# The order of loads, sums and gates in the merged stage of a hybrid attention and convolution layer

## The chip, the cores and the metric

The kernel runs on one core of a Trainium2 chip. The metric is the device time of one execution, in microseconds (us). The engines in the text are TensorE (PE for its products, PEld for its weight loads), VectorE (DVE), ScalarE (ACT), GpSimd (POOL) and SyncE (SP). SP does nothing but start transfers; POOL and ACT start some as well.

## The reference

A block of 256 tokens with 2048 channels goes through one layer: a norm, one wide input projection, two token mixers side by side (attention and a short convolution), two gates, and an output projection with a residual.

```
proj = jnp.einsum('bsd,de->bse', h, w_in)       # q_a, c_kv, k_rope, z_mla, c_in, ..., g_mla, g_conv
attn = attn.reshape(b, s, MLA_WIDTH) * jax.nn.silu(z_mla)
y_mla = jnp.einsum('bse,ed->bsd', attn, w_o_mla)
y_conv = jnp.einsum('bse,ed->bsd', b_gate * conv * jax.nn.silu(z_conv), w_o_conv)
merged = jax.nn.sigmoid(g_mla) * y_mla + jax.nn.sigmoid(g_conv) * y_conv
out = jnp.einsum('bsd,de->bse', merged, w_out)
x = x + _rmsnorm(out, post_norm_g)
```

All data are float32. The change touches what comes after the heads of the attention: the gates g_mla (g_m below) and g_conv (g_c), the products with w_o_mla and w_o_conv, and their merging.

## The kernel before

**Splits.** Every float32 operand is split into a high part, which TensorE takes at its rate for rounded numbers, and a low part, what the rounding left. ACT writes the high part (L252), DVE the low part as a subtraction (L253), and each product is three: high with high, high with low, low with high. On the names: raw is a weight tile as loaded, whi and wlo are its parts (half a tile each, so four instructions per tile), shi and slo are the same for a sum of weight tiles.

**Units.** The merged stage, from about 598 us of the span on, is a list, seq, of units. A unit is a load, a split, products and something that follows them. A plain unit loads one weight tile of 128 x 2048 numbers (1 MiB) by load_raw (L164) and makes 24 products of 128 x 128 by 128 x 512. Each of the four matrices g_m (0), g_c (1), w_o_mla (2) and w_o_conv (3) has four column blocks of four tiles. The tiles are numbered: raw113 to raw116 are g_m's column block 0, raw117 to raw120 g_c's, raw121 to raw136 w_o_mla, then w_o_conv, then the output weights.

**Pairs.** For column blocks 1 to 3 both gates are made together, by paired(c): seven products of half the depth in place of eight, out of sums of weight tiles and of sums of the inputs, called forms. The results stand in three PSUM banks, X, Z and Y, and become four gates: a (g_m, first 128 tokens), b (g_c, first), c (g_c, second) and d (g_m, second). The seven, in order, are Q1 (form 11 into X), V5 (form 5 into Z), V6 (form 6 into X), V7 (form 7), V4 (form 22), V3 (form 3) and Q2 (form 12 into Y). Each has two units of 12 products. The weights of a pair come as tiles b<c>_<matrix>_<tile>. Their sums stand on DVE (L1197): V5 adds b_1_0 and b_1_1 to b_0_0 and b_0_1, V6 adds b_1_2 and b_1_3 to the same, V4 adds b_0_2 and b_0_3. V5 also starts two accumulating transfers on POOL (L1201), which add the tiles 2 and 3 of g_c to b_1_0 and b_1_1 in place; V7 uses these. After V6 ACT copies bank X into sb (L1227); sa, sc and sd are the like for a, c and d.

**Between the pairs** stand plain units of w_o_mla: s1 is Q1, unit 121, V5, unit 122, V6, unit 123, V7, unit 124, V4, 125, 126, V3, 127, Q2, 128. Units 121 to 124 also take in the four blocks of the attention's output. These were written to DRAM and come back transposed as turned90_0 to turned90_3 (L1086); their split is at_both0 to at_both3 on ACT and DVE.

**What sets the order.** seq is walked once. At unit j, loads of up to four units behind it are called, then the splits up to two units behind it, then j's products, then what follows them (copy, sum, sigmoid and the store of a gate, L1026). That only records the work. A scheduler with its own model of times then sets the order in which the instructions stand on each engine; instructions inside tc.keep_in_program_order keep the order of the record. PE's matmuls are all kept. SP's loads of the merged stage are not, so the scheduler may take them in another order than that of seq. Each engine then works through its own list strictly in order. Tiles named raw share three buffers; the tags rt, rb and rc of the pairs' tiles have two each.

**The forms** are made earlier, between the heads of the attention, by make_forms; POOL stores them to DRAM (far_form), and bring_form (L1036) loads them back on SP, in seq, a few units ahead of their use.

Of the kernel before, what the change touches and what calls it, by code (L numbers as in the profile page):

```python
# [82 lines left out]
def tile_layer(ctx: ExitStack, tc: tile.TileContext, xw, w0, xb, x, pos, pvec, post_g, wc, wz, wcv, wkr, wqk, wqr, wv, cwr, wsq, xf, out):  # L83
    nc = tc.nc
# [66 lines left out]
    def load_raw(i):  # L151
# [11 lines left out]
        for a, b, piece in pieces:  # L163
            nc.sync.dma_start(out=t[:, a:b], in_=piece)  # L164
# [664 lines left out]
    def make_forms():  # L829

        kq = KH // 2
        for c in range(2):
# [38 lines left out]
            goes = []  # L871
            for n, src, sign, s in (
                ("11", a11, 1.0, None), ("22", a22, 1.0, None), ("12", a12, 1.0, None), ("5", u, 1.0, (u, a22, a21, ALU.subtract)),
                ("6", w, -1.0, (w, u, a11, ALU.add)), ("7", f7, 1.0, (f7, a11, a21, ALU.subtract)),
                ("3", f3, 1.0, (f3, w, a12, ALU.subtract)),
            ):
# [158 lines left out]
    def bring_form(n):  # L1035
        nc.sync.dma_start(  # L1036
            out=form[n][:, :, :, :].rearrange("p k j c -> p (k j c)").bitcast(F32), in_=far_form[n][:, :]
        )


    seq = []
# [36 lines left out]
    def turned_unit(far, both, first, queue=nc.sync):  # L1078
# [4 lines left out]
        def load():  # L1083
            t = wpool.tile([P, UNIT], F32, name=f"turned{len(seq)}_{first}", tag="raw", bufs=3)
            for i, f in enumerate(far):
                queue.dma_start(out=t[:, i * 1024 : (i + 1) * 1024], in_=f[:, :])  # L1086
            box.append(t)
# [93 lines left out]
    def paired(c):  # L1181
# [133 lines left out]
    s2["Q2"][1][3] = lambda: (gate_last(), branch_last())  # L1315
# [53 lines left out]
    for j in range(len(seq)):  # L1369
        ahead_loads = 0  # L1370
        while nl < len(seq):
            if nl > j and seq[nl][0]:
                pass
# [13 lines left out]
        if j + 3 > len(seq) and done["split"] == u_out[0, 0]:  # L1387
# [3 lines left out]
        if seq[j][2]:  # L1391
            seq[j][2](w)
        if seq[j][3]:
            seq[j][3]()

# [202 lines left out]
```

## Time and profile before

| | us |
|---|---|
| median of 3 runs | 1062.15 |
| lowest and highest | 1062.01 and 1063.28 |
| the profiled execution | 1064.04 |
| its span | 1062.3 |

The span is what the trace covers; 1.7 us of the profiled execution lie outside it. Times in the trace count from the start of the span. "Busy" is the sum of an engine's instructions; a wait row names who waited, for whom, the sum, how often and the longest. PEclk is the clock that TensorE was granted, as a share of the full one.

### The profile page before, as it was taken

What the parts mean: (1) busy time and instruction counts of PE and PEld (TensorE: products, weight loads), DVE (VectorE), ACT (ScalarE), POOL (GpSimd) and SP (SyncE); (2) the same over time, 40 slices, a digit from 0 to 9 for tenths busy, and PEclk for the clock granted to TensorE, in tenths of its full rate; (3) what the DMA queues carried; (4) which work ended last, traced back from release to release, by engine and by line L of the source; (5) the groups of instructions that cost most, each with busy time, mean ns of one, the idle gap of its engine ahead of it and who ended that gap; (6) DMA issues with size and microseconds to landing.
All of it is one profiled execution on the core that took longest, in us unless ns stands there. A gap on an engine that the chain in (4) does not pass through costs nothing.

```text
span 1062.3 us, 12896 instructions
## 1 busy us (share of the span) xinstructions
PE 1020.0 (96%) x4576; PEld 843.5 (79%) x4576; DVE 785.3 (74%) x1074; ACT 580.4 (55%) x811; POOL 200.7 (19%) x366
## 2 busy tenths in 40 slices
PE   9999999999999999999999994799999999998997
PEld 7888888878788788888888873588888778887786
DVE  7588978788677786877767833787988988665662
ACT  7666656546456455564655531565667665433551
POOL 4620322203411223112333201000100102142000
PEclk9999999999999999999999998799999999999999
DMA  9776778759776687756777799578778875687742
GB/s 356 284 240 233 276 230 290 253 192 323 250 273 236 197 292 232 248 200 211 279 248 247 249 403 344 197 285 335 210 247 327 236 286 179 238 309 298 293 179 80
DMA packets 55153, 273.13 MB, mean 257 GB/s; under 512 B 9232, under 2 KB 11920, under 8 KB 30512
## 3 DMA queue, kind: packets, MB, share of 16 engines
q1 hardware_dynamic: 35280, 213.30, 55.3%
q0 software_dynamic: 16784, 50.98, 15.9%
q10 hardware_dynamic: 3024, 8.01, 1.9%
q8 instruction: 36, 0.59, 0.2%
q14 instruction: 29, 0.24, 0.1%
HBM read 239.78 MB, written 28.31 MB: 252 GB/s over the span
## 4 chain that ended last, share of the span: by engine, by line
PE 70%; DMA 15%; DVE 8%; issue 4%; ACT 2%; POOL 1%; DVEq 0%; ACTq 0%; POOLq 0%; SPq 0%
PE cv L88 25%; PE sq L88 15%; PE out L88 6%; DMA raw<-wsq_dram 4%; PE z L88 4%; PE sX L88 4%; DMA form<-far_form 3%; DMA far_form<-form 3%; PE sZ L88 3%; DVE wlo L253 2%; PE qa L88 2%; PE ckv L88 2%; DMA cw<-cwr_dram 2%; PE kn L88 2%; PE qn L88 2%
## 5 line engine op out<-in xcount | busy, mean ns | idle before, releaser
L252 ACT ACTIVATE whi<-raw 128x1024 fp32r<-128x1024 f32 (+1 forms) x318 | 324.3, 1032 | 271.8 <-PE cv L88 97.0
L253 DVE TENSOR_TENSOR wlo<-raw,whi 128x1024 fp32r<-128x1024 f32 (+1 forms) x316 | 371.5, 1191 | 135.3 <-ACT whi L252 129.0
L88 PE MATMUL cv<-whi,x_both 128*128 128x512 f32 x1024 | 320.6, 390 | 2.9 <-DVE vv_lo L253 2.9
L88 PEld LDWEIGHTS cv<-whi,x_both 128*128 128x128 f32 x1024 | 192.7, 188 | 43.4 <-DVE vv_lo L253 3.8
L88 PE MATMUL cv<-wlo,x_both 128*128 128x512 f32 x512 | 200.0, 391 | 0.7 <-DVE wlo L253 0.7
L88 PEld LDWEIGHTS cv<-wlo,x_both 128*128 128x128 f32 x512 | 96.4, 188 | 21.0 <-DVE wlo L253 1.6
L88 PE MATMUL sq<-whi,at_both 128*128 128x512 f32 x256 | 83.3, 398 | 20.4 <-ACT whi L252 20.4
L252 ACT ACTIVATE shi_V<-b 128x1024 fp32r<-128x1024 f32 x60 | 62.6, 1058 | 54.5 <-PE sq L88 33.8
L253 DVE TENSOR_TENSOR slo_V<-b,shi_V 128x1024 fp32r<-128x1024 f32 x60 | 71.8, 1222 | 21.0 <-ACT shi_V L252 20.1
L88 PE MATMUL z<-whi,x_both 128*128 128x512 f32 x256 | 79.9, 389 | 0.0
L88 PE MATMUL sq<-whi,cv_both 128*128 128x512 f32 x256 | 79.9, 389 | 0.0
L88 PEld LDWEIGHTS sq<-whi,at_both 128*128 128x128 f32 x256 | 49.5, 193 | 31.3 <-ACT whi L252 20.8
L338 POOL DMA_DIRECT2D far<-via x64 | 35.4, 559 | 185.6 <-DVE via L330 180.5
L88 PE MATMUL out<-whi,m_both 128*128 128x512 f32 x208 | 66.0, 396 | 1.0 <-ACT whi L252 1.0
L88 PEld LDWEIGHTS sq<-whi,cv_both 128*128 128x128 f32 x256 | 48.1, 188 | 10.0
L88 PEld LDWEIGHTS z<-whi,x_both 128*128 128x128 f32 x256 | 48.1, 188 | 9.9
L88 PE MATMUL sq<-wlo,at_both 128*128 128x512 f32 x128 | 51.2, 400 | 0.5 <-DVE wlo L253 0.5
L88 PE MATMUL sq<-wlo,cv_both 128*128 128x512 f32 x128 | 50.1, 391 | 1.6 <-DVE wlo L253 1.6
L88 PE MATMUL z<-wlo,x_both 128*128 128x512 f32 x128 | 49.8, 389 | 0.0
L88 PEld LDWEIGHTS out<-whi,m_both 128*128 128x128 f32 x208 | 39.8, 191 | 9.7 <-ACT whi L252 1.4
L88 PE MATMUL sX<-shi_V,form 128*128 128x512 f32 x144 | 45.8, 389 | 0.0
L88 PE MATMUL out<-wlo,m_both 128*128 128x512 f32 x104 | 41.3, 397 | 3.9 <-DVE wlo L253 3.9
(281 smaller groups left out, 1578.4 us busy)
## 6 DMA issues: line engine op xcount, KB each, us to landing
raw<-wcv_dram SPq DMA_DIRECT2D x64, 1024.0 KB, 5.9
raw<-wsq_dram SPq DMA_DIRECT2D x56, 1024.0 KB, 6.2
b<-wsq_dram SPq DMA_DIRECT2D x24, 1024.0 KB, 5.4
raw<-wz_dram SPq DMA_DIRECT2D x16, 1024.0 KB, 5.2
raw<-wqk_dram SPq DMA_DIRECT2D x8, 1024.0 KB, 6.5
far_form<-form POOLq DMA_DIRECT2D x14, 512.0 KB, 7.8
form<-far_form SPq DMA_DIRECT2D x7, 1024.0 KB, 18.1
cw<-cwr_dram POOLq DMA_DIRECT2D x24, 256.0 KB, 6.1
```

Of the source, the lines that this page charges most:

```text
L88: return tc.keep_in_program_order(nc.tensor.matmul(*a, **kw))
L252: a = nc.scalar.activation(hi, src, AF.Copy)
L253: b = nc.vector.tensor_tensor(lo, src, hi.bitcast(F32), op=ALU.subtract)
L338: tc.keep_in_program_order(queue.dma_start(out=f[i], in_=m))
```

## The change

It has five parts.

- The loads of the merged stage (weights from g_m's first tile on, forms, pair tiles, and the attention's output) are marked to keep the order of the record on SP.
- In make_forms the sum for the next form is recorded behind the split of the present one.
- New is later(n, fn), which records fn after the products of the n-th unit behind the present one. Sums stay with the unit and the sigmoids that read them on ACT are recorded one unit later. For gate c the sum is recorded one and the sigmoid two units later. The product of the third column block with its gate is recorded two units later.
- The early split of the output weights at the end of the walk may take two tiles, not one.
- Unused lines in the walk go.

```diff
@@ load_raw
-            nc.sync.dma_start(out=t[:, a:b], in_=piece)
+            d = nc.sync.dma_start(out=t[:, a:b], in_=piece)
+            if i >= u_d[0][0][0]:
+                tc.keep_in_program_order(d)
@@ make_forms
-                ("11", a11, 1.0, None), ("22", a22, 1.0, None), ("12", a12, 1.0, None), ("5", u, 1.0, (u, a22, a21, ALU.subtract)),
-                ("6", w, -1.0, (w, u, a11, ALU.add)), ("7", f7, 1.0, (f7, a11, a21, ALU.subtract)),
-                ("3", f3, 1.0, (f3, w, a12, ALU.subtract)),
-            ):
-                if s:
-                    tt(*s)
+                ("11", a11, 1.0, None), ("22", a22, 1.0, None), ("12", a12, 1.0, (u, a22, a21, ALU.subtract)),
+                ("5", u, 1.0, (w, u, a11, ALU.add)), ("6", w, -1.0, (f7, a11, a21, ALU.subtract)),
+                ("7", f7, 1.0, (f3, w, a12, ALU.subtract)), ("3", f3, 1.0, None),
+            )
+            for n, src, sign, following in todo:
                 go = part(n, src, sign)
+                if following:
+                    tt(*following)
@@ bring_form, turned_unit and the pair's load: each dma_start on SP, as here
-                nc.sync.dma_start(out=t[:, :], in_=wsq[n, c, k])
+                tc.keep_in_program_order(nc.sync.dma_start(out=t[:, :], in_=wsq[n, c, k]))
@@
-    seq = []
+    seq, pending, now = [], {}, [0]
+
+    def later(n, fn):
+        pending.setdefault(now[0] + n, []).append(fn)
@@ paired: done_c, done_z, done_y
             copy("c", "X")
-            plus("c", "Z")
-            gate("c", "gc", 1, -1.0)
+            later(1, lambda: plus("c", "Z"))
+            later(2, lambda: gate("c", "gc", 1, -1.0))
...
             plus("b", "Z")
-            gate("b", "gc", 0, -1.0)
+            later(1, lambda: gate("b", "gc", 0, -1.0))
...
             plus("a", "Y")
-            gate("a", "gm", 0, 1.0)
+            later(1, lambda: gate("a", "gm", 0, 1.0))
@@
-    s2["Q2"][1][3] = lambda: (gate_last(), branch_last())
+    s2["Q2"][1][3] = lambda: (gate_last(), later(2, branch_last))
@@ the walk
-        if j + 3 > len(seq) and done["split"] == u_out[0, 0]:
+        now[0] = j
+        while j + 3 - (done["split"] - u_out[0, 0]) > len(seq) and done["split"] < u_out[0, 0] + 2:
...
         if seq[j][2]:
             seq[j][2](w)
+        for fn in pending.pop(j, []):
+            fn()
         if seq[j][3]:
             seq[j][3]()
```

What this does to the engines' lists: PE's and POOL's are the same as before, and all engines have as many instructions as before. The lists of SP, ACT and DVE differ from the gate units of column block 0 on; ahead of that they are the same. Lines of the code shift: L164 stays, L252 and L253 become L254 and L255, L1036 L1039, L1086 L1093, L1189 L1196, L1197 L1204, L1227 L1234.

SP, the loads of the first pair and of the units between its products. Before:

```order
L1189 DMA b1_1_0_5990<-wsq_dram 128x2048
L1189 DMA b1_1_1_6017<-wsq_dram 128x2048
L1036 DMA form_7_5675<-far_form7_643 128x2048
L1189 DMA b1_1_2_6092<-wsq_dram 128x2048
L1189 DMA b1_1_3_6111<-wsq_dram 128x2048
L1036 DMA form_22_5676<-far_form22_644 128x2048
L1086 DMA turned90_0_5914<-far_at0_627 128x1024
L1036 DMA form_3_5677<-far_form3_645 128x2048
L1036 DMA form_12_5678<-far_form12_646 128x2048
L164 DMA raw121_5948<-wsq_dram 128x2048
L1086 DMA turned90_1_6042<-far_at1_628 128x1024
L164 DMA raw122_6054<-wsq_dram 128x2048
```

And the same place now:

```order
L1039 DMA form_6_5674<-far_form6_642 128x2048
L1093 DMA turned90_0_5914<-far_at0_627 128x1024
L164 DMA raw121_5948<-wsq_dram 128x2048
L1196 DMA b1_1_0_5990<-wsq_dram 128x2048
L1196 DMA b1_1_1_6017<-wsq_dram 128x2048
L1039 DMA form_7_5675<-far_form7_643 128x2048
L1093 DMA turned90_1_6042<-far_at1_628 128x1024
L164 DMA raw122_6054<-wsq_dram 128x2048
L1196 DMA b1_1_2_6092<-wsq_dram 128x2048
L1196 DMA b1_1_3_6111<-wsq_dram 128x2048
L1039 DMA form_22_5676<-far_form22_644 128x2048
L1093 DMA turned90_2_6134<-far_at2_629 128x1024
```

The attention's first block and raw121 moved ahead of the g_c tiles b1_1_0 to b1_1_3 and of forms 7, 22, 3 and 12; raw122 moved ahead of b1_1_2 and b1_1_3. Behind the last row follow raw123, turned90_3, raw124, and then b1_0_2, b1_0_3, form 3, raw125, form 12, raw126 and raw127.

ACT, around the copy of bank X after V6 (sb1). Before:

```order
L252 ACTIVATE shi1_V61_1_6152<-b1_0_1_5879 128x1024
L252 ACTIVATE whi123_0_6200<-raw123_6145 128x1024
L252 ACTIVATE whi123_1024_6204<-raw123_6145 128x1024
L252 ACTIVATE shi1_V70_0_6224<-b1_1_0_5990 128x1024
L252 ACTIVATE shi1_V70_1_6228<-b1_1_0_5990 128x1024
L1227 ACTIVATE sb1_6220<-sX1_6004 128x512
L252 ACTIVATE shi1_V71_0_6235<-b1_1_1_6017 128x1024
```

And now:

```order
L254 ACTIVATE shi1_V61_1_6152<-b1_0_1_5879 128x1024
L254 ACTIVATE at_both2_5998<-turned90_2_6134 128x4x128 x2
L1234 ACTIVATE sb1_6220<-sX1_6004 128x512
L254 ACTIVATE whi123_0_6200<-raw123_6145 128x1024
L254 ACTIVATE whi123_1024_6204<-raw123_6145 128x1024
```

sb1 moved from behind the splits of raw123 and of V7's first tile to ahead of raw123's. In the second and third pair it stays where it was. On ACT the sigmoid of the second half of g_c's column block 0 (sg1_0_1), which reads the last product of unit 120, now stands directly ahead of at_both0, and its store (kept_gc_0_1) behind the first split of raw121.

DVE, around V6's first split and V7's last. Before:

```order
L1197 TENSOR_TENSOR b1_0_0_5843<-b1_0_0_5843,b1_1_2_6092 128x2048
L253 TENSOR_TENSOR at_both1_5997<-turned90_1_6042,at_both1_5997 128x4x128
L253 TENSOR_TENSOR slo1_V51_1_6063<-b1_0_1_5879,shi1_V51_1_6062 128x1024
L1197 TENSOR_TENSOR b1_0_1_5879<-b1_0_1_5879,b1_1_3_6111 128x2048
L253 TENSOR_TENSOR wlo122_0_6115<-raw122_6054,whi122_0_6114 128x1024
L253 TENSOR_TENSOR wlo122_1024_6119<-raw122_6054,whi122_1024_6118 128x1024
L253 TENSOR_TENSOR slo1_V60_0_6138<-b1_0_0_5843,shi1_V60_0_6137 128x1024
```

And now, the first of the two places:

```order
L255 TENSOR_TENSOR wlo122_0_6115<-raw122_6054,whi122_0_6114 128x1024
L255 TENSOR_TENSOR wlo122_1024_6119<-raw122_6054,whi122_1024_6118 128x1024
L1204 TENSOR_TENSOR b1_0_0_5843<-b1_0_0_5843,b1_1_2_6092 128x2048
L1204 TENSOR_TENSOR b1_0_1_5879<-b1_0_1_5879,b1_1_3_6111 128x2048
L255 TENSOR_TENSOR slo1_V60_0_6138<-b1_0_0_5843,shi1_V60_0_6137 128x1024
```

And some rows further on the same engine:

```order
L255 TENSOR_TENSOR slo1_V70_1_6229<-b1_1_0_5990,shi1_V70_1_6228 128x1024
L255 TENSOR_TENSOR slo1_V71_0_6236<-b1_1_1_6017,shi1_V71_0_6235 128x1024
L255 TENSOR_TENSOR at_both3_5999<-turned90_3_6180,at_both3_5999 128x4x128 x2
L1204 TENSOR_TENSOR b1_0_0_5843<-b1_0_0_5843,b1_0_2_6222 128x2048
L255 TENSOR_TENSOR slo1_V71_1_6240<-b1_1_1_6017,shi1_V71_1_6239 128x1024
L255 TENSOR_TENSOR wlo124_0_6284<-raw124_6198,whi124_0_6283 128x1024
```

The two sums for V6 moved behind the split of raw122 and stand together ahead of V6's first split. The sum of b1_0_0 with b1_0_2, for V4, stood behind V7's last split and unit 124's first, and stands ahead of V7's last split now. Two more rows moved like these: the sum of b1_0_0 with b1_1_0, for V5, stands ahead of the split of raw121, and the products of the finished columns with their gates (y) stand ahead of a split that came before them.

More of the change, by code (lines that the diff above doesn't have):

```diff
@@ L1035, in bring_form @@
     def bring_form(n):
-        nc.sync.dma_start(
-            out=form[n][:, :, :, :].rearrange("p k j c -> p (k j c)").bitcast(F32), in_=far_form[n][:, :]
-        )
-    seq = []
+        tc.keep_in_program_order(
+            nc.sync.dma_start(
+                out=form[n][:, :, :, :].rearrange("p k j c -> p (k j c)").bitcast(F32), in_=far_form[n][:, :]
+            )
+        )
+    seq, pending, now = [], {}, [0]
+    def later(n, fn):
+        pending.setdefault(now[0] + n, []).append(fn)
     def unit(load=None, split=None, mm=None, after=None):
@@ L1085, in load @@
             for i, f in enumerate(far):
-                queue.dma_start(out=t[:, i * 1024 : (i + 1) * 1024], in_=f[:, :])
+                tc.keep_in_program_order(queue.dma_start(out=t[:, i * 1024 : (i + 1) * 1024], in_=f[:, :]))
             box.append(t)
@@ L1392, in tile_layer @@
             seq[j][2](w)
+        for fn in pending.pop(j, []):
+            fn()
         if seq[j][3]:
             seq[j][3]()
+    assert not pending
     last_m = turned_unit(far_m[3:4], m_b, 3, nc.gpsimd)
```

6 lines of the change are left out of this document (1 added, 5 removed).

## The prediction

> **What bounds the kernel now.** I read the shares of the engines first, then the waits of PE, then the chain of waits, then the timelines around the place that these name.
>
> ```profile
> PE 1020.0 (96%) x4576; PEld 843.5 (79%) x4576; DVE 785.3 (74%) x1074; ACT 580.4 (55%) x811; POOL 200.7 (19%) x366
> ...
> PE sq L88 <- ACT whi L252: 20.4, 1, 20.4
> ...
> 671.79 8.14 PE sq L88 x23
> 679.94 5.44 PE sZ L88 x24
> ```
>
> PE is busy 96% of 1062.3 us, and the change leaves its products and their order alone. So the time can only come from PE's gaps, and one wait of 20.4 us is nearly half of the 42.3 us in which PE stands still. The last two rows give the unit of all that follows: 24 products at full rate take 5.44 us, 0.227 each. The 23 after the wait took 8.14.
>
> ```profile
> 641.04 28.30 DMA raw<-wsq_dram
> ...
> 642.53 0.39 PE L88 MATMUL sX<-shi_Q,form 128*128 128x512 f32 x1
> 670.53 0.80 PE L88 MATMUL sq<-whi,at_both 128*128 128x512 f32 x1 [20.39 <-ACT whi L252]
> 679.77 0.39 PE L88 MATMUL sZ<-shi_V,form 128*128 128x512 f32 x1
> ```
>
> The wait is for the split of raw121, the first unit of w_o_mla. Its load was issued at 641.04, 1.5 us before Q1 began, and needed 28.3 us. What made it late and then slow stands in the timeline of SP and the shares of the DMA queues:
>
> ```profile
> 592.61 17.93 SPq L164 DMA_DIRECT2D raw<-wsq_dram  x4
> ...
> 632.76 0.33 SPq L1036 DMA_DIRECT2D form<-far_form  x1
> 633.19 0.41 SPq L1086 DMA_DIRECT2D turned<-far_at  x1
> 635.51 3.06 SPq L1036 DMA_DIRECT2D form<-far_form  x2
> 614.00:646.00 32.00, 31.37 (x139) 25.66 (x138) 14.19 (x11) 11.50 (x13) 0.96 (x1) 1.00 1.01 420
> 656.00:664.00 8.00, 0.00 (x0) 0.00 (x0) 1.18 (x2) 0.37 (x1) 0.00 (x0) 0.50 1.03 292
> q0 software_dynamic: 148, 1.07, 63.3%
> q1 hardware_dynamic: 149, 1.09, 33.7%
> ```
>
> The window rows give length, busy time of PE, PEld, DVE, ACT and POOL, the granted clock, the DMA share and GB/s. From 614 to 646 the DMA is full at 420 GB/s, which is 2.5 us for each 1 MiB tile (1.05 MB). From 656 to 664 (queue rows: packets, MB, share of time) SP's loads, q1, moved only 1.09 MB in 8 us, 0.136 MB/us. The other half went to POOL's two accumulating transfers, q0.
>
> **The change part by part.** The edit of the forms' maker and the second early split of the output weights move no instruction; they cost nothing. What moves is SP's order, and with it the order in which ACT and DVE stand.
>
> *1. The stall.* raw121 now stands on SP directly behind form 6, ahead of four g_c tiles and forms 7, 22, 3, 12. raw119 is the last of the four loads in the first row of SP, so it goes out at 592.61 + 17.93 - 0.33 = 610.2. From it to raw121 come raw119, form 5, raw120, b1_0_0, b1_0_1, form 6, half a tile of attention and raw121 itself, 7.5 MiB: 7.5 x 2.5 = 18.7 us. So it is in by 629 to 640, before Q1 starts, even if a wait for a buffer lies between. Without the wait V5's first product (sZ) would stand two units behind Q1, at 642.53 + 10.88 = 653.41; it stood at 679.77. That is 26.4 us: the wait, two short ones in Q1 and the slow products. A small wait ahead goes as well:
>
> ```profile
> 620.63 1.05 ACT L252 ACTIVATE whi<-raw 128x1024 fp32r<-128x1024 f32 x1
> 630.30 0.33 ACTq L1026 DMA_DIRECT2D kept_gm<-sg  x1
> 633.11 0.50 PE L88 MATMUL sq<-wlo,x_both 128*128 128x512 f32 x1 [0.63 <-DVE wlo L253]
> ```
>
> ACT's store of the gate stood 9 us at its issue for a g_c tile; in the new order what precedes it is raw118, long landed: 0.6. Together **-27.0**.
>
> *2. u121.* Its low part on DVE now stands behind the sum into b1_0_0. Of that sum's 2.29 us the part that lies beside other work is not to be seen in this trace: at 0 to 2.3 I take a third, since Q1's 5.44 still run when at_both0 is split: **+0.7**.
>
> *3. V6's sums.* V6's first split stands behind both its sums on DVE, so it needs b1_1_2 and b1_1_3. These queue on SP behind raw122, which takes the buffer of the first attention tile and so waits for that tile's split:
>
> ```profile
> 640.01 0.69 ACT L1107 ACTIVATE sg<-sq,r_both 128x512 f32<-128x512 f32 x1 [1.66 <-PE sq L88]
> 655.22 1.15 ACT L252 ACTIVATE at_both<-turned 128x512 fp32r<-128x512 f32 x2 [4.45 <-DMA turned<-far_at]
> 657.21 0.33 SPq L164 DMA_DIRECT2D raw<-wsq_dram  x1
> 642.58 0.96 POOL L1201 DMA_DIRECT2D b<-wsq_dram  x1 [32.38 <-DVE b L1197]
> L1197 DVE TENSOR_TENSOR b<-b,b x6: 2284/2289/2293, 639.5 to 707.5; 128x2048 f32<-128x2048 f32 x6
> L253 DVE TENSOR_TENSOR slo_V<-b,shi_V x16: 1216/1220/1227, 672.8 to 714.3; 128x1024 fp32r<-128x1024 f32 x16
> DMA to landing us min/median/max: 4.7/6.3/28.3
> b<-wsq_dram POOLq DMA_DIRECT2D x6, 1024.0 KB, 12.7
> ```
>
> ACT's at_both0 stands behind the second sigmoid (sg), which reads the last product of the gate's last unit. That product now ends at 642.53 - 0.63 = 641.9; with 0.3 to the reading and 0.6 for it, at_both0 begins at 642.8. From there to the load of raw took 657.21 - 655.22 = 1.99, so raw122 goes out at 644.8. b1_0_0's sum follows on DVE and ends 2.29 later, at 647.1, where POOL's first accumulating transfer starts; two of them at 12.7 us each share the DMA until about 672. SP thus has the full 0.42 MB/us for 2.3 us (0.97 MB) and then 0.136. The three tiles, 3.15 MB, need 2.18 / 0.136 = 16.0 us after that, and with 4.7 - 2.5 = 2.2 us from issue to the first byte b1_1_3 lands at 647.1 + 2.2 + 16.0 = 665.3. Its sum (2.29) and V6's low part (1.22) end at 668.8. V6 is due four units after Q1 and term 2: 641.9 + 0.7 + 4 x 5.44 = 664.4. **+4.4**. Bounds: 1.0, when the tiles are early and DVE alone is late; 7.0, if SP gets somewhat less of the DMA.
>
> *4. The gate's copy.* sb1 on ACT reads V6's last product and now stands ahead of unit 123's splits; before it stood behind them.
>
> ```profile
> 696.29 0.60 ACT L1227 ACTIVATE sb<-sX 128x512 f32<-128x512 f32 x1 [0.29 <-PE sX L88]
> ```
>
> PE has nothing between: 0.3 + 0.6 + 1.06 (a split on ACT) = 1.9 without a product, then 1.22 for the low part less the two products that come first, 1.1 at most. **+3.0** (1.9 to 3.5).
>
> *5. V7's last split* on DVE now stands behind the sum of b1_0_0 with b1_0_2, whose load gets its buffer only from V7's second split. After term 4 DVE begins unit 123's low part as PE reaches the unit, and V70_1's low part ends about three splits later, 3 x 1.22 = 3.7. From there load 4.7 + sum 2.29 + split 1.22 = 8.2, ending at 11.9. V7's last quarter is due 5.44 + 3 x 1.36 = 9.5 after the unit's start (a half of a pair's tile is 6 products, 1.36): **+2.4** (0, if DVE gets ahead again, to 3.6, if the load takes 1.2 longer).
>
> *6. The clock* after these waits.
>
> ```profile
> 278.14 0.58 PE L88 MATMUL sc<-kn,qn_hi 128*128 128x256 f32 x1 [2.05 <-DVE kn L253]
> 279.00:282.00 3.00, 3.00 (x10) 2.43 (x10) 2.06 (x7) 0.66 (x2) 2.77 (x6) 0.58 1.01 321
> ```
>
> A wait of 2.05 us was followed by 3 us at 0.58, a loss of 1.3; the wait of 0.63 inside 614 to 646 left that window at 1.00. Three waits of 2 to 4 us can cost 0 to 4.5; I take one loss and a part of another: **+1.7**.
>
> [...]
>
> *7. Later.* V4 waits for a sum with b1_0_3 that is loaded in one batch with five others: 0 to 3.5 (sum and split). The products with the gates (y) now stand ahead of low parts in three columns:
>
> ```profile
> 712.54 0.69 DVE L1132 TENSOR_TENSOR y<-sq,y 128x512 f32<-128x512 f32 x1
> 680.00:760.00 80.00, 80.00 (x354) 66.28 (x353) 68.22 (x60) 51.21 (x54) 4.90 (x8) 1.00 0.73 266
> ```
>
> Two of 0.69 each time: 0 to 4.2 in all. Before, PE had no gap at all from 680 to 760 with DVE busy 85%, since the long stall had let DVE and the loads run ahead; that lead is gone. Half of 7.7: **+3.9**.
>
> **Sum:** -27.0 + 0.7 + 4.4 + 3.0 + 2.4 + 1.7 + 3.9 = -10.9. The profiled execution took 1064.04 (span 1062.3); 1053.1 then. It lies 1.9 above the median of 1062.15, so the forecast is **1051 us**.
>
> **Rivals.** *Smaller gain* (under 6 us, about 1058): terms 3 to 7 near their upper ends. For it: the DMA share of 0.73 after 680 leaves little to catch up with. Against: not all ends can meet, since a wait at V6 gives time to what comes after.
>
> *Larger gain* (over 16, about 1045): the tiles of term 3 are early and only DVE's 1.0 is left, no clock loss (-27.0 + 0.7 + 1.0 + 3.0 + 2.4 = -19.9, of which the later waits take 3). Against: the half rate of q1 in 656 to 664 is measured, and the accumulating transfers still come then.
>
> *No change:* the wait for raw121 only becomes one for b1_1_3 of like length. That needs all upper ends: 2.3 + 7.0 + 3.5 + 3.6 + 4.5 + 7.7 = 28.6.
>
> *Slower:* one mechanism, the batch behind V7's last split. Its release lets six loads go together, and what is needed first shares the DMA with what is needed last. At 292 GB/s instead of 420, 5 MiB take 18.0 instead of 12.5 us, 5.5 more for PE to wait, and this in all three columns: 16.5, so -10.9 + 16.5 = +5.6, about 1068. It decides once accumulating transfers overlap that batch; in the first column they should be over by 672, and V7 comes later.
>
> *That the order does not change* is excluded by the rows of SP shown above: raw121 stands nine places earlier.
>
> **How the numbers follow.** Forecast (6 to 16 us faster) 0.72; larger 0.06; smaller but clear 0.10; no change 0.04; slower 0.08. This kernel's measurements tell about 0.2% (2 us) from nothing. Faster: 0.72 + 0.06 + 0.10 = 0.88. The range from 1046 to 1058 holds the forecast and part of the smaller gains; term 3's and term 7's bounds alone make some 3 to 4 us either way.
>
> **What would show it.** Right: raw121 issued near 622 to 632, no wait of 20 us, raw122 issued near 645 after a gap on SP, then a wait of some 4 us before V6 for slo_V, 3 in two pieces before unit 123 behind sb, 2 to 3 in V7; the store of the gate at 620 not waiting. Step 3 is wrong if b1_1_3 lands before 660, step 6 if the clock stays at 1.00 through 664 to 690. The whole is wrong if any new wait is over 10 us, or if the gain comes from elsewhere than 633 to 680.

## The result

The changed kernel took 1047.27 us (median of 4 runs, 1046.46 to 1049.99) beside 1062.72 for the kernel before: a ratio of 0.9847, 95% interval 0.9805 to 0.9888. That is 15.5 us less; forecast were 1051 and a range of 1046 to 1058. In a later comparison the same kernel took 1053.87 beside 1063.38, a ratio of 0.9908 (0.9882 to 0.9934), 9.5 us less. Where these 6 us between two comparisons come from is a part of what follows.

The waits of PE after the change, whole execution (who waited, for whom: us in total, times, longest):

```profile
PE sq L88 <- ACT whi L254: 4.4, 1, 4.4
PE out L88 <- DVE wlo L255: 3.1, 1, 3.1
PE cv L88 <- DVE vv_lo L255: 3.1, 2, 1.8
PE sq L88 <- DVE wlo L255: 2.1, 4, 0.8
...
PE sX L88 <- DVE slo_V L255: 1.6, 3, 0.8
PE sX L88 <- ACT shi_V L254: 1.1, 1, 1.1
```

The wait of 20.4 us ahead of unit 121 is gone. One of 4.4 us stands in its place, two units of w_o_mla later, and a few of about 1 us are new. SP's timeline shows the new order at work, and PE's the two ends of the new wait:

```profile
621.83 0.33 SPq L1093 DMA_DIRECT2D turned<-far_at  x1
627.27 0.33 SPq L164 DMA_DIRECT2D raw<-wsq_dram  x1
...
645.16 0.33 SPq L164 DMA_DIRECT2D raw<-wsq_dram  x1
645.55 0.90 SPq L1196 DMA_DIRECT2D b<-wsq_dram  x2
646.62 0.53 SPq L1039 DMA_DIRECT2D form<-far_form  x1
649.64 0.33 SPq L1093 DMA_DIRECT2D turned<-far_at  x1
657.67 0.33 SPq L164 DMA_DIRECT2D raw<-wsq_dram  x1
```

```profile
642.40 0.39 PE L88 MATMUL sX<-shi_Q,form 128*128 128x512 f32 x1
647.84 0.39 PE L88 MATMUL sq<-whi,at_both 128*128 128x512 f32 x1
664.75 0.39 PE L88 MATMUL sX<-shi_V,form 128*128 128x512 f32 x1
675.42 0.50 PE L88 MATMUL sq<-whi,at_both 128*128 128x512 f32 x1 [4.41 <-ACT whi L254]
684.88 0.39 PE L88 MATMUL sX<-shi_V,form 128*128 128x512 f32 x1
```

raw121 is issued at 627.27 instead of 641.04, and unit 121 begins at 647.84, right behind Q1's 5.44. The load of 657.67 is raw123, and unit 123, at 675.42, waits for it. On ACT the copy sb1 was done by 672.0, and the split of raw123 then waited 2.3 us more, for the load:

```profile
671.44 0.58 ACT L1234 ACTIVATE sb<-sX 128x512 f32<-128x512 f32 x1
674.31 2.01 ACT L254 ACTIVATE whi<-raw 128x1024 fp32r<-128x1024 f32 x2 [2.30 <-DMA raw<-wsq_dram]
```

The products of that unit then run slowly: from 675.42 to V7 at 684.88 are 9.46 us, for 5.44 of work and a wait of 0.8. The granted clock says so (length; busy time of PE, PEld, DVE, ACT, POOL; PEclk; DMA share; GB/s):

```profile
668.00:676.00 8.00, 3.52 (x15) 2.35 (x13) 2.75 (x4) 3.32 (x5) 0.00 (x0) 1.00 1.03 406
676.00:680.00 4.00, 3.32 (x8) 2.64 (x9) 4.00 (x5) 4.00 (x6) 0.00 (x0) 0.50 0.11 45
680.00:684.00 4.00, 4.00 (x14) 3.13 (x13) 2.38 (x4) 0.51 (x2) 0.00 (x0) 0.66 0.69 254
684.00:690.00 6.00, 6.00 (x28) 4.97 (x27) 5.10 (x4) 4.74 (x5) 0.00 (x0) 1.00 0.16 27
```

The difference of the two executions can be followed along PE's list, since its order is the same in both. Each row gives when a piece of work began on PE's timeline.

| work begins | before | after | after - before |
|---|---|---|---|
| Q1, first pair | 642.53 | 642.40 | -0.1 |
| V5 | 679.77 | 653.87 | -25.9 |
| V6 | 690.65 | 664.75 | -25.9 |
| unit 123 | 696.09 | 675.42 | -20.7 |
| V7 | 701.53 | 684.88 | -16.7 |
| second pair (Q1) | 750.49 | 735.13 | -15.4 |
| third pair, V7 | 860.10 | 844.66 | -15.4 |
| unit behind it | 865.54 | 854.15 | -11.4 |
| output products | 959.71 | 947.65 | -12.1 |
| last step | 1054.05 | 1039.77 | -14.3 |

So 25.9 us were won at one place, 9.2 given back between V6 and V7 of the first pair, 4.6 more up to the output products, and 2.2 won there. The last 2.2 are no gain of the change: that stretch varies between executions of one kernel, as the last experiment shows.

### The profile page after: what moved, and what is told of

Read it like the earlier page. It is cut to its first block, busy times and chain, and to the rows that moved or that the text cites. A ratio compares the mean times of both kernels' runs of the same rounds, so it can differ in the third digit from the quotient of the medians.

```text
span 1048.2 us, 12876 instructions
## 1 busy us (share of the span) xinstructions
PE 1022.9 (98%) x4576; PEld 845.2 (81%) x4576; DVE 784.4 (75%) x1074; ACT 580.0 (55%) x811; POOL 200.3 (19%) x366
## 4 chain that ended last, share of the span: by engine, by line
PE 72%; DMA 13%; DVE 9%; issue 4%; ACT 2%; POOL 1%; SPq 0%; DVEq 0%; POOLq 0%; ACTq 0%
PE cv L88 28%; PE sq L88 15%; PE out L88 8%; PE z L88 4%; DMA raw<-wsq_dram 3%; DMA b<-wsq_dram 3%; PE qa L88 2%; DMA far_form<-form 2%; PE sX L88 2%; DVE wlo L255 2%; PE ckv L88 2%; PE kn L88 2%; PE qn L88 2%; DVE slo_V L255 1%; DMA cw<-cwr_dram 1%
## 5 line engine op out<-in xcount | busy, mean ns | idle before, releaser
L255 DVE TENSOR_TENSOR wlo<-raw,whi 128x1024 fp32r<-128x1024 f32 (+1 forms) x316 | 371.8, 1192 | 134.8 <-ACT whi L254 128.6
L254 ACT ACTIVATE whi<-raw 128x1024 fp32r<-128x1024 f32 (+1 forms) x318 | 324.1, 1032 | 267.3 <-PE cv L88 98.4
L254 ACT ACTIVATE shi_V<-b 128x1024 fp32r<-128x1024 f32 x60 | 61.9, 1057 | 59.7 <-PE sq L88 26.0
L255 DVE TENSOR_TENSOR slo_V<-b,shi_V 128x1024 fp32r<-128x1024 f32 x60 | 71.2, 1222 | 19.4 <-ACT shi_V L254 19.0
L340 POOL DMA_DIRECT2D far<-via x64 | 35.4, 559 | 181.1 <-DVE via L332 178.0
L88 PEld LDWEIGHTS sq<-whi,at_both 128*128 128x128 f32 x256 | 49.5, 193 | 15.4 <-ACT whi L254 5.1
```

Source lines behind the costliest of these rows:

```text
L88: return tc.keep_in_program_order(nc.tensor.matmul(*a, **kw))
L254: a = nc.scalar.activation(hi, src, AF.Copy)
L255: b = nc.vector.tensor_tensor(lo, src, hi.bitcast(F32), op=ALU.subtract)
L340: tc.keep_in_program_order(queue.dma_start(out=f[i], in_=m))
```

## The experiments

Each kernel ran beside the kernel before on the same chip. The stretch from Q1's first product to V7's in the first pair, read from PE's timeline, is the measure for the first pair; its products alone take 6 x 5.44 = 32.6 us. Four comparisons followed the first, each with its own runs of the kernel before: raw121's place alone, copy moved back, form 22 later, and both of these moves in one; marks alone, no accumulating transfers, third pair first, and all three moves in another; the two repeats in the third; the two kernels with gb and xr later in the fourth.

| kernel | median us | ratio to before (95%) | Q1 to V7 |
|---|---|---|---|
| before | 1062.72 | | 59.0 |
| changed | 1047.27 | 0.9847 (0.9805 to 0.9888) | 42.5 |
| changed, once more | 1053.87 | 0.9908 (0.9882 to 0.9934) | 42.6 |
| marks alone | 1051.26 | 0.9889 (0.9862 to 0.9915) | 41.6 |
| raw121's place alone | 1051.45 | 0.9885 (0.9846 to 0.9925) | 43.3 |
| copy moved back | 1050.75 | 0.9883 (0.9853 to 0.9914) | 42.3 |
| form 22 later | 1042.61 | 0.9801 (0.9774 to 0.9829) | 38.7 |
| form 22 later, once more | 1045.23 | 0.9831 (0.98 to 0.9862) | 36.9 |
| form 22 later and copy back | 1042.92 | 0.98 (0.9772 to 0.9828) | 36.2 |
| no accumulating transfers, first pair | 1041.39 | 0.9787 (0.976 to 0.9814) | 35.4 |
| third pair's transfers first | 1049.03 | 0.9864 (0.984 to 0.9888) | 42.8 |
| all three moves | 1043.25 | 0.9814 (0.979 to 0.9839) | 38.3 |
| gb and xr later | 1051.61 | 0.9859 (0.9821 to 0.9896) | 41.7 |
| form 22, gb and xr later | 1043.82 | 0.9794 (0.9763 to 0.9824) | 36.9 |

### Which part of the change acts

Three parts of the change were built alone. With the edit of the forms and the second early split, every engine's list is that of the kernel before, row for row. With these and the later sums and gates, but no marks on the loads, it is the same again. With nothing but the marks the lists and the waits in them are those of the changed kernel. So the marks on the loads are the whole change; the recorded places of the sums and sigmoids move nothing, because the scheduler orders ACT and DVE by its own times. The marks alone were run, this one and the like for forms, pair tiles and turned blocks:

```diff
-            nc.sync.dma_start(out=t[:, a:b], in_=piece)
+            d = nc.sync.dma_start(out=t[:, a:b], in_=piece)
+            if i >= u_d[0][0][0]:
+                tc.keep_in_program_order(d)
```

> The kernel before with nothing but the marks on the loads of the merged stage; sums, gates, forms and the early split as before. Its instructions stand on each engine in the same order as those of the changed kernel. Theory (the marks are the whole change): the time of the changed kernel, 1046 to 1050, and the same waits in the trace, 4.4 ahead of unit 123 among them. Rival (the recorded places of sums and gates count by the waits they are given): over 3 us away from it.

The median was 1051.26, more than 3 us from the first time of the changed kernel, but between its two. In the trace the waits are the same: 4.3 ahead of unit 123, then 0.5, and 0.8 at unit 126. Since the two are one program, the spread between comparisons is some 4 to 6 us, and medians of different comparisons that lie closer than that don't tell their kernels apart. Nor do ratios that lie within 0.006, since those of this one program run from 0.9847 to 0.9908. What tells kernels apart is a pair of medians of one comparison, and the stretch Q1 to V7, which took 41.6, 42.5 and 42.6 us in three profiled executions of this program.

> The changed kernel once more, beside the next one on the same chip. The kernel with the marks alone has the same instructions in the same order with the same waits and took 1051.3, the changed kernel 1047.3 in another comparison. Theory (the two are one program, and the difference is the spread between comparisons): 1046 to 1052, 11 to 17 us under before.

It took 1053.87, over the expected 1052. Its waits say where it lost:

```profile
PE sq L88 <- ACT whi L254: 4.7, 1, 4.7
PE out L88 <- DVE wlo L255: 4.4, 3, 3.1
PE out L88 <- ACT whi L254: 4.2, 1, 4.2
```

The wait for raw123 is there as before (4.7). A second one of 4.2 in the output products is new; the last experiment is on it. From Q1 to the first output product the two profiled executions of the changed kernel took 305.3 and 304.2 us, 11.9 and 13.0 less than before, so the change itself did the same in both. The difference lies outside that stretch: the second began Q1 2.2 us earlier, and its output products took 7.2 us longer.

### raw121's place alone

The kernel before, with marks on raw121, the first turned block and the pair tiles of column block 1 only:

```diff
-            nc.sync.dma_start(out=t[:, a:b], in_=piece)
+            d = nc.sync.dma_start(out=t[:, a:b], in_=piece)
+            if i == u_d[0][2][0]:
+                tc.keep_in_program_order(d)
...
+                if both is at_b and first == 0:
+                    tc.keep_in_program_order(d)
...
+                if c == 1:
+                    tc.keep_in_program_order(d)
```

> The kernel before, with only the first block of the attention, raw121 and the first pair's tiles kept in the order of the record. On SP raw121 now stands ahead of the four g_c tiles, but behind all seven forms, 4 MiB more than in the changed kernel. Theory (the gain is raw121's place ahead of the g_c tiles and of POOL's accumulating transfers): 11.5 MiB from 610 at 2.5 us each put raw121 in by 640 to 646; the wait of 20.4 us ahead of unit 121 falls to 0 to 3, V5 begins near 654 to 657 instead of 679.8, and the time falls by 12 to 22 us. Rival (the whole new order is needed, forms included): the wait stays above 8 us and the time within 8 us of before.

The wait fell to 2.7, as expected, the time by 11.3 us, a little less than the 12 to 22 that were named and more than the rival's 8. V5 began only at 664.40, not between 654 and 657: Q1 itself began 4.5 us later than in the kernel before, and from Q1 to V5 are 17.3 us, 37.2 before. The forms that stand ahead kept raw121 from being in time, and the short wait was followed by slow products as well, 9.06 us from the unit's start to V5 (655.34 to 664.40), with a second wait of 0.47 in it, for 5.44 of work:

```profile
647.07 0.39 PE L88 MATMUL sX<-shi_Q,form 128*128 128x512 f32 x1
655.34 0.80 PE L88 MATMUL sq<-whi,at_both 128*128 128x512 f32 x1 [2.67 <-ACT whi L254]
677.61 0.39 PE L88 MATMUL sX<-shi_V,form 128*128 128x512 f32 x1
```

So raw121's place ahead of the g_c tiles is most of the gain. On balance the rest of the new order adds nothing that could be measured here, 43.3 us from Q1 to V7 against 42.5, though the losses lie elsewhere: this kernel loses at raw121 and in the three units behind it, the changed one at raw123.

### What holds unit 123

By the prediction the copy sb1 on ACT holds unit 123; by the trace after, raw123. Three kernels tell the two apart, all of them made from the changed one. In the first the copy is kept behind V7's first split:

```diff
-            nc.scalar.activation(res[name][:, :], banks[b][:, :], AF.Copy)
+            a = nc.scalar.activation(res[name][:, :], banks[b][:, :], AF.Copy)
+            if keep:
+                tc.keep_in_program_order(a)
...
-            ("V6", (0, 0), None, (1, 2), "6", "X", False, False, lambda: copy("b", "X")),
+            ("V6", (0, 0), None, (1, 2), "6", "X", False, False, lambda: later(2, lambda: copy("b", "X", c == 1)) if c == 1 else copy("b", "X")),
...
+                    if c == 1 and name == "V70":
+                        tc.keep_in_program_order(first)
```

> The changed kernel with one instruction moved: the first pair's copy of bank X on ACT stands behind V7's first split again. By the prediction's term 4 the wait ahead of unit 123 is this copy's, and the time falls by 1.9 to 3.5 us. By the trace of the changed kernel raw123 lands only at 674.2, so the copy is hidden behind its load: within 1 us of the changed kernel, and the wait stays at 4.4.

In the second form 22 is loaded with unit 123, behind raw123:

```diff
-    for name, n in (("Q1", "6"), ("V5", "7"), ("V6", "22"), ("V4", "3")):
+    for name, n in (("Q1", "6"), ("V5", "7"), ("V4", "3")):
         with_form(s1[name][1], n)
+    with_form(p[0][2], "22")
```

> The changed kernel with the load of form 22 moved on SP from behind b1_1_3 to behind raw123. Theory (unit 123's wait of 4.4 us is the late landing of raw123, behind form 22 on a DMA that is shared with two accumulating transfers): raw123 lands near 669.4 instead of 674.2. Then the copy of bank X on ACT, which stands ahead of raw123's split, is what is left: a wait of 2.0 for ACT and 0.8 for DVE. Time 2.4 to 4 us under the changed kernel. Rival (the copy alone sets the wait): no change, within 1 us, and the wait stays at 4.4.

The third has both edits:

> As the run with form 22 moved, and the first pair's copy of bank X also put behind both halves of V7's first split on ACT, where it stood before the change. Theory: neither raw123 nor the copy holds unit 123; no wait there, the clock stays at 1.00 through 664 to 690. From V6 to V7's first product the changed kernel loses 25.90 - 16.65 = 9.25 us; 7 to 9 of them come back, time 1038 to 1041. Rival (something else is late next, V7's sums or V4): less than 4 us better than the changed kernel.

The copy alone changed nothing: 1050.75, between the times of the changed kernel, and the same wait of 4.41. So the copy does not set the wait there. With form 22 out of the way the time fell by 8.6 us against the changed kernel on the same chip (1045.23 and 1053.87 in the repeat, intervals of the ratios apart), more than the 2.4 to 4 first expected, and what was left at unit 123 is the copy. The edit moves more than the load: on DVE the scheduler now also puts V7's last split ahead of the sum for V4. That split comes after V7's first product, outside the stretch Q1 to V7. ACT of the kernel with form 22 later:

```profile
668.73 0.60 ACT L1234 ACTIVATE sb<-sX 128x512 f32<-128x512 f32 x1 [2.61 <-PE sX L88]
669.23 1.99 ACT L254 ACTIVATE whi<-raw 128x1024 fp32r<-128x1024 f32 x2
```

```profile
670.33 0.50 PE L88 MATMUL sq<-whi,at_both 128*128 128x512 f32 x1 [1.63 <-ACT whi L254]
```

sb waits for V6's last product, the split stands behind it, and PE waits 1.63 and then 0.76 for the low part. With the copy moved back as well PE waited 0.55 and 0.76, and Q1 to V7 took 36.2. That is still 3.6 above the products alone, so "no wait" was too much; the clock stayed at 1.00 as expected. The time, 1042.92, missed the 1038 to 1041 expected and is not to be told from the 1042.61 of the kernel with form 22 later alone.

> The changed kernel with form 22 loaded behind raw123, beside the changed kernel on the same chip. Theory (raw123's late landing costs the wait and the slow products behind it): 4 to 9 us under the changed kernel of this comparison, outside both intervals. Rival (the difference between the first comparisons was spread): within 2 us.

The gain over the changed kernel was 8.6 us, at the upper end of the 4 to 9 expected. By Q1 to V7 it is 42.6 - 36.9 = 5.7, and that part is form 22's. In the two profiled executions the output products add 7.2, from the changed kernel's wait of 4.2 and what follows it, and a Q1 that began 4.2 later takes that much away; no run links these to form 22. Two more pairs of one comparison, without and with form 22 later, lie 7.8 us apart each (1050.75 and 1042.92, both with the copy back; 1051.61 and 1043.82, below), with 6.1 and 4.8 in the stretch. So the gain is there in all three, 4.8 to 6.1 of it where it was looked for; where the rest comes from is open.

### Why raw123 is late

The changed kernel without the two transfers of the first pair:

```diff
                     k = plus[1]
-                    tc.keep_in_program_order(
-                        nc.gpsimd.dma_start(out=raw[1, k][:, :], in_=wsq[1, c, 2 + k], accum_op=ALU.add)
-                    )
+                    if c != 1:
+                      tc.keep_in_program_order(
+                          nc.gpsimd.dma_start(out=raw[1, k][:, :], in_=wsq[1, c, 2 + k], accum_op=ALU.add)
+                      )
```

> The changed kernel without the first pair's two accumulating transfers of POOL, so the third and fourth tiles of g_c are missing from V7's weights there. The copy of bank X stands behind V7's first split in this build, which the run with the copy moved alone has shown to be worth nothing. In the changed kernel the stretch from Q1's first product to V7's first takes 42.5 us where the products alone take 32.6. Theory (raw123 is late since those transfers take half of the DMA): raw123 lands within 7 us of its issue instead of 16.6, the stretch takes 33 to 34.5, no wait over 1 us in it, the time falls by 7 to 10 us. Rival (form 22 and the place in SP's queue alone make it late): the stretch stays above 38.

The time from issue to landing of raw123 (the one load in the window), first in the changed kernel, then with form 22 later, then without the accumulating transfers:

```profile
DMA to landing us min/median/max: 16.6/16.6/16.6
```

```profile
DMA to landing us min/median/max: 13.1/13.1/13.1
```

```profile
DMA to landing us min/median/max: 4.7/4.7/4.7
```

So POOL's transfers are the cause, and the place behind form 22 costs 3.5 us while they run. Without them it costs nothing: form 22 landed at 655.3, before raw123 was issued at 656.3. Two small loads of POOL, the gates of 256 KB each that stood behind the transfers, are gone from this place too; they were issued at 625.6 and 628.7. This kernel leaves two of g_c's tiles out of V7's weights, so it shows a cost and is no way to save it. There was no wait for a load in the stretch; 0.9 for DVE's sums at V6 and two waits of 0.3 stayed, which made it 35.4 instead of the expected 33 to 34.5. The time was 1041.39, 9.9 us under the marks alone on the same chip, inside the 7 to 10 expected.

### The third pair

The product of the third column block with its gate is recorded later, which puts its stores on POOL behind the third pair's transfers:

```diff
-    s2["Q2"][1][3] = lambda: (gate_last(), later(2, branch_last))
+    s2["Q2"][1][3] = lambda: (gate_last(), later(6, branch_last))
```

> The changed kernel with the third column's product with its gate recorded six units later instead of two, so that on POOL the third pair's accumulating transfers stand ahead of the two stores of that product. Theory (the loss of 4.05 us in the third pair's V7, 9.49 instead of 5.44, is the second accumulating transfer, issued late behind those stores and landing at 847.5): V7 there takes 5.4 to 7, and the time falls by 2 to 4 us. Rival (DVE's sums hold these transfers, not the stores): V7 there still takes 9 or more.

V7 there took 5.44, and PE waited for nothing in it. But the loss moved one unit ahead instead of going: the unit before it now waited 1.9 and 0.7 for its low parts and took 8.6. DVE's rows there say why:

```profile
837.55 0.69 DVE L1139 TENSOR_TENSOR y<-sq,y 128x512 f32<-128x512 f32 x1 [2.39 <-DMA y<-kept_gm]
838.16 1.21 DVE L255 TENSOR_TENSOR wlo<-raw,whi 128x1024 fp32r<-128x1024 f32 x1
```

The product with the gate (y) stands ahead of the unit's low part, and it waited 2.4 us for its gate. POOL loads that gate back, and this load now stands behind the transfers (issued at 831.5, landed at 837.5; in the changed kernel it was in by 822.7). From the second pair's Q2 to the third's the execution took 84.9 us; ten executions of the changed kernel and of kernels made from it without this move took 85.3 to 87.6 (changed kernel 86.8 and 85.4). The median of 1049.03 lies 2.2 under that of the marks alone, inside the spread. So the place of V7's loss was right, and that the move mends it is not shown.

> Form 22 behind raw123, the copy of bank X behind V7's first split, and the third pair's accumulating transfers ahead of the stores. Theory: the gains add, 4 to 5 us from the first pair's stretch and 2 to 4 from the third pair's V7 on top: 1036 to 1040. Rival (what is won in the third pair is lost at the output product behind it): as the kernel without the third move, 1041 to 1043.

The gains did not add: 1043.25, as the kernel without the third move (1042.92), as the rival had it, but not for the rival's reason: the third pair's loss moved one unit ahead, as with the third move alone (waits of 2.5 and 0.7). In its execution the first pair's stretch took 38.3 us, and from the second pair's Q2 to the third's 88.1.

### The output products

The changed kernel's two profiled executions took 92.1 and 99.3 us from the first output product to the last step. In the longer one POOL's request for the last merged block (turned, L1093) came 0.1 us behind ACT's 2 MiB for xr; in the other it came 3.5 us ahead of it. From issue to landing, the shorter execution first:

```profile
L1093 POOL DMA_DIRECT2D turned<-far_m x1: 577/577/577, 955.1 to 955.1; - x1
...
DMA to landing us min/median/max: 3.8/3.8/3.8
```

```profile
L1093 POOL DMA_DIRECT2D turned<-far_m x1: 582/582/582, 960.4 to 960.4; - x1
...
  ACT m_both L254: 10.2, 1
...
DMA to landing us min/median/max: 12.6/12.6/12.6
```

Two kernels, the changed one and that with form 22 later, got gb and xr behind that block's split:

```diff
-    nc.scalar.dma_start(out=gb[:, :], in_=post_g.to_broadcast([P, D]))
-    nc.scalar.dma_start(out=xr[:, :, :], in_=x)
...
         out_products(pss[c], w, kk)
+        if i == 1:
+            tc.keep_in_program_order(nc.scalar.dma_start(out=gb[:, :], in_=post_g.to_broadcast([P, D])))
+            tc.keep_in_program_order(nc.scalar.dma_start(out=xr[:, :, :], in_=x))
```

> The changed kernel with two transfers on ACT's queue in the output stage moved: the gains (gb, 1 MiB) and the tokens (xr, 2 MiB) stand behind the split of the last merged block instead of two splits ahead of it. In the two profiles of the changed kernel the stretch from the first output product to the last step took 92.1 and 99.3 us: in the slow one the last merged block was asked back at 960.4, 0.1 us after xr, and needed 12.6; in the other at 955.1, before it, and needed 3.8. Theory (this race is a good part of the spread between executions and comparisons): that stretch takes 91 to 93, the wait of 4.2 for the block's split does not come, and the time lies 2 to 6 us under 1053.9, with a spread under 4 us. Rival (the spread comes from the stages ahead): the spread stays at 5 us or more and the median at 1049 to 1054.

> Both moves that showed something: form 22 behind raw123, and gb and xr behind the last merged block's split. Theory: 1039 to 1043, the stretch Q1 to V7 36 to 39 us and the output stretch 91 to 93. Rival (the loads of gb and xr now meet the last weights): the output stretch 94 or more, 1045 or more.

The stretch took 91.7 and 93.3 us in these two (the second a little over the 91 to 93 expected), and the wait for the block's split did not come. The time of the second, 1043.82, lies a little over the 1039 to 1043 expected too. That the move mends the longer case is not shown, since one execution of each kernel was profiled, and the slow landing alone does not make the longer case. In 9 of the 12 profiled executions in which gb and xr stand where they were, the kernel before among them, the request came within 0.2 us of xr's, and the block took 11.8 to 12.7 us to land; in eight of these the stretch still took only 92.1 to 94.3. In those eight the request came 10.9 to 13.2 us after the first output product, in the longer execution 16.0. So the slow landing hurts when the request is late as well; why it was late there was not followed.

The spread did not shrink: 1045.7 to 1054.0 in the first, median 1051.61, as the rival had it. A part of it lies ahead of the merged stage, whose first pair began anywhere between 638.3 and 647.1 us in the profiled executions of all kernels. The same two places of PE's timeline, first in an early execution (form 22 later and copy back; it has no wait at the first place), then in a late one (gb and xr later):

```profile
361.21 0.50 PE L88 MATMUL cv<-whi,x_both 128*128 128x512 f32 x1 [0.62 <-DVE vv_lo L255]
```

```profile
224.96 0.50 PE L88 MATMUL cv<-whi,x_both 128*128 128x512 f32 x1 [2.88 <-DVE vv_lo L255]
...
367.62 0.79 PE L88 MATMUL cv<-whi,x_both 128*128 128x512 f32 x1 [2.86 <-DVE vv_lo L255]
```

Two waits for the split of the values, at about 222 and 364 us, take 0 to 2.9 us each in these two executions. Neither this change nor any of the experiments touches them.

The best of the kernels that compute the whole layer are those with form 22 behind raw123: 1042.6, 1045.2 and, with gb and xr later, 1043.8 in three comparisons. Their ratios, 0.979 to 0.983, lie below both of the changed kernel's; what carries the comparison are the three pairs of one comparison above.

## Why the prediction was right, and where not

The forecast of -10.9 us in the profiled execution met -14.05 (1064.04 to 1049.99) in the first and -10.2 (to 1053.87) in the second; the range held both. The first median, 1047.27, lies 1.3 us from the range's end. The mechanism of the gain and its price, term 1, were right; that the sum of the losses came near is luck, because its errors partly cancelled. Terms 3 and 5 were 4.0 and 2.4 us too high, terms 4, 6 and 7 were 2.2, 1.6 and 0.7 too low. Term by term, by the table along PE's list:

| term | predicted | measured | |
|---|---|---|---|
| 1 stall of unit 121 | -27.0 | -27.3 | right |
| 2 unit 121's low part | +0.7 | +0.6 | right |
| 3 V6's sums | +4.4 | +0.4 | wrong |
| 4 unit 123 | +3.0 | +5.2 | right place, wrong cause |
| 5 V7's last split | +2.4 | 0 | hidden behind term 6 |
| 6 slow clock | +1.7 | +3.3 | one loss instead of parts of three |
| 7 later | +3.9 | +4.6 | right size, two places |
| output products | none | -2.2 | of this execution, not of the change |

With the 0.8 us by which the merged stage began later in this execution, the measured column adds up to -14.6; the last step came 14.3 earlier, and the rest is rounding and small waits.

*Term 1.* raw121 landed at 635.7, inside the forecast's 629 to 640, and V5 begins 25.9 us earlier. With the 0.6 of term 2 and those 0.8 the stall's removal is 27.3. On SP raw121 stands eight places earlier, not nine as the prediction counts; nothing hangs on it. The store of the gate no longer waits at its issue: it was issued at 621.56, right behind its sigmoid, which ended at 621.53.

*Term 3* failed at its start of the accumulating transfer. It took 2.2 us from issue to the first byte, the estimate it had made for SP's loads. The first one was issued at 648.1, and from 648 to 652 only SP's queue moved anything (first row below; queue: packets, MB, share of time). q0 first shows between 652 and 653, and from 660 to 668 (the other two rows) the two share as predicted:

```profile
q1 hardware_dynamic: 209, 1.57, 102.0%
...
q0 software_dynamic: 180, 1.14, 65.8%
q1 hardware_dynamic: 184, 1.17, 36.4%
```

So about 4 us pass before it moves its first byte. In that time raw122 and b1_1_2 came in at 0.39 MB/us (1.57 MB in 4 us), and b1_1_3 met the sharing alone; it landed at 660.5, where 665.3 was forecast. The trace before has the same lag, and the term could have been priced with it: there the first transfer was issued at 642.58, and q0 moved nothing until 646. DVE's row says that V6's two sums ran without a wait between them:

```profile
659.83 4.49 DVE L1204 TENSOR_TENSOR b<-b,b 128x2048 f32<-128x2048 f32 x2
```

PE waited 0.4 us. The lower bound of the term, 1.0 for DVE alone, was the right case: without the transfers the same place waited 0.9.

*Term 4.* The place, unit 123, and the sign were right; the cause was not. The sharing that term 3 charged to b1_1_3 fell on raw123, which waits on SP for the buffer of the second attention block (its split ended at 657.64, raw123 was issued at 657.67) and then queues behind form 22 (it landed at 674.2). The prediction never asked for the landing of the next load in that queue. Its price for the copy, 1.9 for ACT and 1.1 for DVE, was nearly met once raw123 was early: 1.63 and 0.76.

*Term 5.* The sum ahead of V7's last split did wait 2.5 us for its load, and the split was done 12.9 us after unit 123's start; the forecast had 11.9. But it was due at 13.5 and not at 9.5, because the unit took 9.46 us instead of 5.44, with its wait of 0.8 and its slow products. So term 6 hid term 5. In the kernels with form 22 later the split stands ahead of that sum, so they can't show the term by itself.

*Term 6.* The 1.7 was the author's estimate for three waits, from the one that the trace before showed, 1.3 lost behind 2.05 us; the upper end of 4.5, 1.5 for each of the three, is an estimate too. Of the waits in the changed kernel only the one of 4.4 was followed by a lower clock in the first pair: 0.50 from 676 to 680 and 0.66 from 680 to 684. With form 22 later the shorter one of 1.63 was, in one execution and not in the other, the window behind the wait each time:

```profile
672.00:676.00 4.00, 4.00 (x12) 3.12 (x11) 4.00 (x5) 3.10 (x5) 0.00 (x0) 0.57 0.51 183
```

```profile
676.00:680.00 4.00, 3.99 (x17) 3.30 (x18) 4.00 (x4) 3.52 (x5) 0.00 (x0) 1.00 0.54 229
```

Q1 to V7 took 38.7 in the first and 36.9 in the second, 1.7 apart, with the same wait. So the same wait cost about 1.7 more in one execution than in the other; what decides it was not shown. With all three moves a wait of only 1.0 was followed by clocks of 0.77 and 0.80 in two windows of 4 us, again 1.7 lost.

*Term 7.* Between the first pair's V7 and the output products 4.0 us were lost at the third pair's V7, which waited 1.1 for ACT and 0.8 for DVE and ran at a lower clock (0.75 from 848 to 852, 0.82 from 852 to 856). It waited for the second accumulating transfer of that pair, which POOL starts behind two stores (issued at 831.4, landed at 847.5). The products with the gates, for which the term was made, cost nothing that shows; the batch ahead of V4 cost 1.3 at unit 126 (a wait of 0.8 among it). Behind the third pair's V7 0.7 came back, since the unit there had a wait of 1.4 before. In the second profiled execution that V7 took 7.5 us and the unit behind it 7.1, and the whole stretch lost 3.4.

*The rivals.* "No change, the wait only moves" came true in kind, not in size: from raw121 to raw123, 20.4 to 4.4. The slower case, the batch behind V7's last split, was too small to matter. The larger gain (over 16) did not come, though the first comparison came within 0.6 us of it. Its condition, that term 3's tiles are early, did hold; the transfers of POOL then held back raw123 in their place.

## What to carry to other kernels

When a queue is put in order of need, work out the landing of every load behind the reordered one, up to the first that has slack, not only of the one that was late; here the wait moved from raw121 (20.4 us) to raw123 (4.4), a load that shared the DMA with POOL's accumulating transfers. A load that is needed late (form 22 here, 1 MiB) belongs behind those that are needed sooner (raw123, as large), even where the order of the program says otherwise: the move took Q1 to V7 from 42.6 to 36.9 us. Before trusting the parts of a change, compare the order of instructions with each part alone: of this one's parts only the marks moved anything.

## What the runs showed that was not expected

- An accumulating transfer of 1 MiB on POOL's queue moved its first byte about 4 us after its issue, and while it ran, SP's loads fell from 420 GB/s to about 146 (1.17 MB in 8 us).
- A 512 KB load on POOL's queue that was issued within 0.2 us of a 2 MiB load on ACT's, before or behind it, took 11.8 to 12.7 us in nine executions; issued 3.3 to 3.6 us ahead of it, 3.8 to 4.0 in three.
- A wait of 1.6 us was followed by 4 us at a clock of 0.57 in one execution and at 1.00 in two others of the same stretch, a difference of 1.7 us; one of 1.0 was followed by a like loss (0.77 and 0.80).
- The same kernel's gain over the one before was 15.5 us in one comparison and 9.5 in another. Waits ahead of the change, for the split of the values, and one behind it, in the output products, come and go between executions.
